# Unread products of ones behind the routing tables of the second and third token tile

## The chip, the cores and the metric

One core of a Trainium2 chip runs the whole program. The metric is the time of one execution on the device in microseconds, given as the median of several runs. Beside these runs there is one profiled execution, whose trace the rows below come from. All matrix products run on TensorE (PE in the profile); VectorE (DVE), ScalarE (ACT) and GpSimd (POOL) do the rest, and SyncE (SP) issues most transfers.

## What is computed

Two transformer blocks run one after the other on 512 tokens of width 1024. The first has a recurrent layer and a sliding-window layer, the second an mLSTM with a Fourier mixer. What this change touches is the end of the second block, where a hierarchical mixture of experts begins:

```
g_logits = h @ w_router_group + b          # 4 groups
g_sel    = argmax(g_logits)
e_sel    = (h @ w_router_expert + b) of that group    # 4 experts of it
top_v, top_i = top_k(e_sel, 2)
...
for e in range(16):
    a = silu(h @ w_gate[e]) * (h @ w_up[e])
    y = y + combine[..., e] * (a @ w_down[e])
```

The reference runs every expert on every token and weighs the results. The kernel computes each expert on the tokens routed to it alone, so it must first know the routes.

## The kernel before

The 512 tokens stand in four tiles of 128, t = 0 to 3. The stage around the change lies between the output projection of the mixer and the first expert.

`finish(t)` ends a tile of the mixer: it scales and adds the residual (line 1416, into `x3[t]`), lets ScalarE sum the squares of the result (line 1417), and for t below 3 transposes `x3[t]` on TensorE in two halves (`logits`, line 1398, copied out by ScalarE at line 1399) and multiplies it by the router's weights (line 1401). Of tile 3 most of this product was made earlier; what is left is one half of its `y`, transposed at the same line 1398. `finish(t)` also lets `h2(t - 1)` write the previous tile's rows to memory (line 1440), and makes the product with a row vector at line 1424. Last it calls `route`.

`route(t)` is a chain of some 30 small VectorE operations on the 20 logits of each token: it ranks groups and experts (lines 1567 to 1584), then TensorE counts how many earlier tokens went to each expert, in one group of three products (lines 1587, 1588 and 1589; the last, `self.ranked`, needs what line 1581 made). VectorE reads the count (line 1593), makes the one-hot rows by which the first expert's tokens are picked (line 1594) and two pairs of one-hot tables (lines 1609 and 1611), and two products at line 1612 add them into `self.tp`, the table of places. `self.tp` takes eight products over the four tiles.

After the third tile's ranks, `pick` (line 1546) multiplies the rows of tiles 0 to 2 by their one-hot rows, and after the fourth's those of tile 3: 32 products that give the first expert its tokens, already transposed. ScalarE and VectorE split them (lines 294 and 295), and the first expert's matrix products start (lines 303 to 305). The finished table gives the addresses (lines 1617 to 1619) by which the second expert's tokens are gathered from memory (line 1514). From then on 16 experts follow, each with three products per weight piece.

`warm(n)` makes n products of a 128x128 tile of ones with itself repeated (128x256 each), which nobody reads. It is used elsewhere in the program, where TensorE waits. `issue_after` asks the scheduler to place instructions behind a given one. The scheduler, not the code alone, decides in which order each engine's instructions stand.

Of the kernel before, what the change touches and what calls it, by code (L numbers as in the profile page):

```python
# [9 lines left out]
F32 = mybir.dt.float32  # L10
# [8 lines left out]
P = 128  # L19
T = 512  # L20
# [251 lines left out]
class Kern:  # L272
# [32 lines left out]
        self.last = mm(ps, lhsT=wl, rhs=xh, start=False, stop=stop)  # L305
        return self.last

    def warm(self, n, tag="at"):

        after = self.last  # L310
        ps = self.pps.tile([P, T], F32, name=tag, bufs=2)
        with self.tc.issue_after(after.ins):
            for _ in range(n):
                self.last = self.nc.tensor.matmul(ps[:, :2 * P], lhsT=self.ones,
                                                  rhs=self.ones[:, None, :].to_broadcast([P, 2, P]), start=True, stop=True)
# [1235 lines left out]
    def route(self, pc, lg, t):  # L1551

        nc = self.nc
        g, e = lg[:, 0:4], lg[:, 4:20].rearrange("p (g j) -> p g j", j=4)
        w = pc.tile([P, 153], F32, name="rtw", bufs=2)
        n = [0]

        def tw(*sh):
            k = math.prod(sh)
            n[0] += k  # L1560
            o = w[:, n[0] - k:n[0]]
            return o.rearrange("p (a b) -> p a b", a=sh[0]) if len(sh) == 2 else o

        def rank(x):

            d, r = tw(4, 4), tw(4)
            nc.vector.tensor_sub(d, x[:, None].to_broadcast([P, 4, 4]), x[:, :, None].to_broadcast([P, 4, 4]))
            nc.vector.tensor_tensor(d, d, self.c3("tie").rearrange("p (a b) -> p a b", a=4), op=ALU.is_gt)
            nc.vector.reduce_sum(r, d, axis=AX.X)
            return r  # L1570

        es, s = self.es[:, t], self.s12[:, t]
        gsel, em, s12 = tw(4), tw(4, 4), tw(4)
        nc.vector.tensor_scalar(gsel, rank(g), 0.0, None, op0=ALU.is_equal)
        gb = gsel[:, :, None].to_broadcast([P, 4, 4])
        nc.vector.tensor_mul(em, e, gb)
        nc.vector.reduce_sum(es, em.rearrange("p g j -> p j g"), axis=AX.X)
        r = rank(es)
        nc.vector.tensor_scalar(s12, r, 2.0, None, op0=ALU.is_lt)
        AA, A = tw(16), tw(2, 16)  # L1580
        nc.vector.tensor_mul(AA.rearrange("p (g j) -> p g j", j=4), gb, s12[:, None, :].to_broadcast([P, 4, 4]))
        for k in range(2):
            nc.vector.tensor_scalar(s[:, k], r, float(k), None, op0=ALU.is_equal)
            nc.vector.tensor_mul(A[:, k].rearrange("p (g j) -> p g j", j=4), gb, s[:, k, None, :].to_broadcast([P, 4, 4]))

        rp = self.pps.tile([P, 16], F32, name="mm", bufs=self.mmb)
        nc.tensor.matmul(rp, lhsT=self.ones, rhs=self.cum[:, t], start=True, stop=False)
        nc.tensor.matmul(rp, lhsT=self.ones[0:1], rhs=self.c3("eb")[0:1], start=False, stop=False)
        self.ranked = nc.tensor.matmul(rp, lhsT=self.c3("lt"), rhs=AA, start=False, stop=True)
        nc.vector.tensor_add(self.cum[:, t + 1], self.cum[:, t], AA)  # L1590

        p0 = tw(1)
        nc.vector.tensor_copy(p0, rp[:, 0:1])
        self.picked = nc.vector.tensor_scalar(self.oh0[:, t], self.c3("i128"), p0, AA[:, 0:1], op0=ALU.is_equal, op1=ALU.mult)
        m, val, rf = tw(2, 16), tw(2), tw(2, 2)
        nc.vector.tensor_mul(m, A, rp[:, None].to_broadcast([P, 2, 16]))
        ri = pc.tile([P, 3, 2], I32, name="ri", bufs=2)
        pos = tw(2)
        nc.vector.reduce_sum(pos, m, axis=AX.X)
        nc.vector.tensor_copy(ri[:, 0], pos)  # L1600
        nc.vector.tensor_scalar(ri[:, 1], ri[:, 0], 7, None, op0=ALU.logical_shift_right)
        nc.vector.tensor_scalar(ri[:, 2], ri[:, 0], P - 1, None, op0=ALU.bitwise_and)
        nc.vector.tensor_copy(rf, ri[:, 1:3])
        nc.vector.tensor_sub(val, self.c3("dest")[:, 2 * t:2 * t + 2], pos)

        oh = pc.tile([P, 2, 192], F32, name="oh", bufs=2)
        ohc, ohr = oh[:, :, :P], oh[:, :, P:]
        for k in range(2):
            nc.vector.tensor_scalar(ohr[:, k], self.c3("i64"), rf[:, 0, k:k + 1], val[:, k:k + 1], op0=ALU.is_equal,
                                    op1=ALU.mult)  # L1610
            nc.vector.tensor_scalar(ohc[:, k], self.c3("i128"), rf[:, 1, k:k + 1], None, op0=ALU.is_equal)
            nc.tensor.matmul(self.tp, lhsT=ohc[:, k], rhs=ohr[:, k], start=t + k == 0, stop=t + k == 4)

    def places(self):

# [460 lines left out]
```

## Time and profile before

| What | Value |
|---|---|
| median of 3 runs | 1872.26 us (1869.57 to 1874.68) |
| profiled execution, time | 1876.02 us |
| profiled execution, span of the trace | 1874.2 us |
| TensorE busy | 95% of the span |
| VectorE, ScalarE, GpSimd busy | 66%, 45%, 17% |
| mean granted clock of TensorE | 0.971 of full speed |

The span is what the trace covers, from the first instruction to the last; 1.8 us of the profiled time lie around it. The granted clock is 1.00 at TensorE's upper level of 2.4 GHz and 0.50 at the lower one of 1.2 GHz.

### The profile page before, as it was taken

How to read it: one execution, taken by the hardware profiler on the slowest of the kernel's cores; microseconds unless marked ns; L12 is line 12 of the kernel's file. 1: busy time of each engine (PE TensorE's matmuls, PEld its weight loads, DVE VectorE, ACT ScalarE, POOL GpSimd, SP SyncE). 2: the span in 40 equal slices, each digit the busy share in tenths (PEclk: the TensorE clock that was granted, in tenths of full speed). 3: DMA queues.
4: the chain of work that ended last, by engine and by line, in shares of the span. 5: the costliest groups of instructions: out<-in, count | busy, mean ns of one | idle time of the engine just before them, and what ended most of it. 6: DMA issues, size and time to landing. Idle time of an engine off the chain costs nothing.

```text
span 1874.2 us, 22970 instructions
## 1 busy us (share of the span) xinstructions
PE 1788.7 (95%) x8590; PEld 1447.1 (77%) x8590; DVE 1244.0 (66%) x2316; ACT 842.6 (45%) x1505; POOL 323.1 (17%) x251
## 2 busy tenths in 40 slices
PE   7899999999999999999999999988999889999995
PEld 5678788888888777777888888877877778888873
DVE  7854666577567665466645656568475698897897
ACT  6643432223234343434313222446454456786774
POOL 2300200000002100032000000222100024454543
PEclk9899999999999899999999999989999989999998
DMA  5212124334435411122343343301115359898883
GB/s 190 90 68 90 68 90 145 126 115 147 155 127 177 141 46 46 57 73 93 135 157 113 132 145 112 111 23 63 46 52 213 135 225 370 334 342 355 346 351 148
DMA packets 55257, 278.83 MB, mean 149 GB/s; under 512 B 7346, under 2 KB 16738, under 8 KB 28130
## 3 DMA queue, kind: packets, MB, share of 16 engines
q1 hardware_dynamic: 38146, 173.48, 26.6%
q0 software_dynamic: 16992, 103.82, 14.3%
q8 instruction: 69, 1.13, 0.2%
q14 instruction: 50, 0.41, 0.1%
HBM read 259.96 MB, written 17.32 MB: 148 GB/s over the span
## 4 chain that ended last, share of the span: by engine, by line
PE 83%; DVE 9%; ACT 2%; issue 1%; POOL 1%; DMA 1%; ACTq 0%; POOLq 0%; DVEq 0%
PE mm L303 22%; PE mm L305 22%; PE mm L304 22%; PE ax L641 2%; PE ax L396 1%; PE at L607 1%; PE ax L1749 1%; PE ax L625 1%; DVE h L453 1%; PE mm L1546 1%; PE dn L304 1%; PE ax L1401 1%; DVE elo L1509 1%; PE dn L303 0%; PE mm L986 0%
## 5 line engine op out<-in xcount | busy, mean ns | idle before, releaser
L303 PE MATMUL mm<-xh,whi 128*128 128x512 f32 x912 | 367.4, 404 | 11.6 <-ACT whi L294 8.1
L294 ACT CAST whi<-wraw 128x512 fp32r<-128x512 f32 x356 | 199.8, 607 | 395.6 <-DMA wraw<-w_fi_in 160.7
L304 PE MATMUL mm<-xl,whi 128*128 128x512 f32 (+1 forms) x944 | 373.9, 396 | 3.1 <-DVE xl L299 2.3
L295 DVE TENSOR_TENSOR wlo<-wraw,whi 128x512 fp32r<-128x512 f32 x352 | 240.3, 715 | 199.8 <-ACT whi L294 188.4
L305 PE MATMUL mm<-xh,wlo 128*128 128x512 f32 x912 | 363.0, 399 | 1.7 <-DVE wlo L295 1.7
L303 PEld LDWEIGHTS mm<-xh,whi 128*128 128x128 f32 x912 | 174.3, 191 | 56.7 <-ACT whi L294 9.8
L304 PEld LDWEIGHTS mm<-xl,whi 128*128 128x128 f32 x944 | 180.3, 191 | 44.5 <-DVE xl L299 4.5
L305 PEld LDWEIGHTS mm<-xh,wlo 128*128 128x128 f32 x912 | 174.1, 191 | 40.7 <-DVE wlo L295 2.9
L304 PE MATMUL mm<-al,whi 128*128 128x512 f32 (+1 forms) x520 | 201.1, 387 | 0.0
L303 PE MATMUL mm<-ah,whi 128*128 128x512 f32 x480 | 190.0, 397 | 0.7 <-ACT ah L294 0.7
L305 PE MATMUL mm<-ah,wlo 128*128 128x512 f32 x480 | 188.8, 394 | 0.0
L1509 DVE TENSOR_TENSOR elo<-wr,ehi 128x1024 fp32r<-128x1024 f32 x104 | 126.1, 1223 | 45.3 <-ACT ehi L1508 42.8
L440 POOL TENSOR_TENSOR acc<-acc,tmp 128x512 f32<-128x512 f32 (+1 forms) x50 | 67.0, 1339 | 434.1 <-ACT tmp L438 432.7
L304 PE MATMUL mm<-elo,X 128*128 128x512 f32 x352 | 138.6, 394 | 1.7 <-DVE elo L1509 1.5
L303 PE MATMUL mm<-ehi,X 128*128 128x512 f32 x352 | 138.0, 399 | 0.7 <-ACT ehi L1508 0.7
L305 PE MATMUL mm<-ehi,X 128*128 128x512 f32 x352 | 138.2, 393 | 0.0
L1508 ACT CAST ehi<-wr 128x1024 fp32r<-128x1024 f32 x104 | 108.7, 1052 | 61.5 <-PE mm L305 58.4
L515 POOL TENSOR_TENSOR tmp<-tmp 128x512 f32<-128x512 f32 x20 | 29.8, 1488 | 592.7 <-ACT tmp L509 437.2
L304 PEld LDWEIGHTS mm<-al,whi 128*128 128x128 f32 x520 | 99.3, 191 | 19.4 <-issue 0.8
L924 DVE SCALAR_TENSOR_TENSOR tmp<-wraw,silc,tmp 128x256 f32<-128x256 f32 x224 | 111.8, 532 | 1.9
L303 PEld LDWEIGHTS mm<-ah,whi 128*128 128x128 f32 x480 | 90.9, 190 | 23.1 <-issue 1.9
L305 PEld LDWEIGHTS mm<-ah,wlo 128*128 128x128 f32 x480 | 91.1, 190 | 19.6 <-issue 0.7
(550 smaller groups left out, 3131.3 us busy)
## 6 DMA issues: line engine op xcount, KB each, us to landing
wraw<-w_fi_in SPq DMA_DIRECT2D x44, 1024.0 KB
wraw<-w_ada_in SPq DMA_DIRECT2D x24, 1024.0 KB
wraw<-w_fo_in SPq DMA_DIRECT2D x16, 896.0 KB
wr<-w_ex_in SPq DMA_DIRECT2D x12, 1024.0 KB
wraw<-w_out_in SPq DMA_DIRECT2D x8, 1024.0 KB
wraw<-w_fo_in SPq DMA_DIRECT2D x8, 1024.0 KB
wraw<-w_in_a_in SPq DMA_DIRECT2D x5, 1024.0 KB
wraw<-w_mem_in SPq DMA_DIRECT2D x4, 1024.0 KB
```

The lines of the kernel that those rows point to most:

```text
L294: ins = nc.scalar.copy(hi, src)
L295: (eng or nc.vector).tensor_sub(lo, src, hi.bitcast(F32))
L303: mm(ps, lhsT=wh, rhs=xh, start=start, stop=False)
L304: mm(ps, lhsT=wh, rhs=xl, start=False, stop=False)
L305: self.last = mm(ps, lhsT=wl, rhs=xh, start=False, stop=stop)
L396: self.last = nc.tensor.matmul(ps[:, j * na + n:j * na + n + 1], lhsT=acc[:, j * P:(j + 1) * P], rhs=self.ones[:, 0:1], start=True, stop=True)
L440: nc.gpsimd.tensor_add(accs[0], accs[0], s)
L515: (nc.gpsimd if j % 2 else nc.vector).tensor_mul(t, t, gt.pop(j))
L641: nc.tensor.matmul(yb[:, n, r], lhsT=pts[n // 2][:, r, n % 2, b], rhs=x, start=b == vs[0][0], stop=b == 1)
L924: nc.vector.scalar_tensor_tensor(t, raw[:, k], s, t, op0=ALU.mult, op1=ALU.add)
L1508: self.split_hi = self.nc.scalar.copy(hi, src)
L1509: (eng or self.nc.vector).tensor_sub(lo, src, hi.bitcast(F32))
```

## The change

`route` now notes its last table product, and calls `warm` behind the tables of tiles 1 and 2 with six and eight products. They write a tile of the pool "mm" instead of "at", and `warm` takes the number of that pool's buffers.

```diff
-    def warm(self, n, tag="at"):
+    def warm(self, n, tag="at", bufs=2):
 
         after = self.last
-        ps = self.pps.tile([P, T], F32, name=tag, bufs=2)
+        ps = self.pps.tile([P, T], F32, name=tag, bufs=bufs)
         with self.tc.issue_after(after.ins):
             for _ in range(n):
                 self.last = self.nc.tensor.matmul(ps[:, :2 * P], lhsT=self.ones,
...
             nc.vector.tensor_scalar(ohc[:, k], self.c3("i128"), rf[:, 1, k:k + 1], None, op0=ALU.is_equal)
-            nc.tensor.matmul(self.tp, lhsT=ohc[:, k], rhs=ohr[:, k], start=t + k == 0, stop=t + k == 4)
+            self.last = nc.tensor.matmul(self.tp, lhsT=ohc[:, k], rhs=ohr[:, k], start=t + k == 0, stop=t + k == 4)
+        if t in (1, 2):
+            self.warm(4 + 2 * t, "mm", self.mmb)
```

Lines behind it have numbers two higher in the changed kernel. The order of instructions changes with it. On TensorE, behind the table of tile 0 (the first row), this is the difference; X_10742 is `x3[2]`, the products at line 1401 are the logits, L314 are the ones:

```order
 L1612 MATMUL ax<-oh 128x64 x2
+L1589 MATMUL mm<-rtw,cst_10714 128x16
+L1612 MATMUL ax<-oh 128x64 x2
+L314 MATMUL mm<-ones 128x256 x6
 L1398 MATMUL mm<-cst,X_10742 128x128 x8
+L1587 MATMUL mm<-acc_72,ones 128x16
+L1588 MATMUL mm<-cst_10714,ones 128x16
 L1401 MATMUL ax<-wrg,xg 128x20 x8
 L1589 MATMUL mm<-rtw,cst_10714 128x16
```

The rank product and the table of tile 1, which stood behind tile 2's transposes and logits, now stand ahead of them, and the six ones with them. The last row is the rank product of tile 1 before the change, and of tile 2 after it.

Behind that row TensorE goes on as follows; X_10813 is `y`, whose transposes belong to the logits of tile 3:

```order
+L1612 MATMUL ax<-oh 128x64 x2
+L314 MATMUL mm<-ones 128x256 x8
+L1398 MATMUL mm<-cst,X_10813 128x128 x4
 L1587 MATMUL mm<-acc_72,ones 128x16
 L1588 MATMUL mm<-cst_10714,ones 128x16
-L1398 MATMUL mm<-cst,X_10813 128x128 x4
+L1546 MATMUL mm<-oh_10822,X_10813 128x128 x3
 L1401 MATMUL ax<-wrg,xg 128x20 x4
-L1612 MATMUL ax<-oh 128x64 x2
+L1546 MATMUL mm<-oh_10822,X_10813 128x128 x21
 L1589 MATMUL mm<-rtw,cst_10714 128x16
```

Here the table of tile 2 and the eight ones stand ahead of the transposes and logits of tile 3, which before the change came ahead of the table of tile 1. The picks of tiles 0 to 2 (L1546) follow.

On VectorE this is the difference behind the third tile's one-hot rows; L1427 and L1428 take up the logits of tile 3, L376 to L380 are the small operations of its norm:

```order
 L1611 TENSOR_SCALAR oh<-cst_10714,rtw 128x128
+L1427 TENSOR_TENSOR lg<-lg,ax 128x20
+L1428 SCALAR_TENSOR_TENSOR lg<-lg,st,ax 128x20
+L1424 TENSOR_TENSOR X_10813<-X_10743,row 128x1024
+L376 TENSOR_SCALAR st<-st 128x1
+L377 RECIPROCAL st<-st 128x1
+L378 TENSOR_TENSOR st<-st 128x1
+L379 SCALAR_TENSOR_TENSOR st<-st 128x1
+L380 SCALAR_TENSOR_TENSOR st<-st 128x1
 L1434 SCALAR_TENSOR_TENSOR lg<-lg,st,cb 128x20
 L1440 SCALAR_TENSOR_TENSOR X_10813<-X_10813,st,row_10816 128x1024
```

These eight operations stood inside tile 2's route before; now they come behind it.

## Rows read from the trace of the kernel before

**Rows 1.** The page: the span, and TensorE's busy time, share and instructions.

```profile
span 1874.2 us, 22970 instructions
PE 1788.7 (95%) x8590; PEld 1447.1 (77%) x8590; DVE 1244.0 (66%) x2316; ACT 842.6 (45%) x1505; POOL 323.1 (17%) x251
```

**Rows 2.** Stretches, TensorE alone: length, busy (instructions), granted clock, DMA share, GB/s.

```profile
1487.50:1490.60 3.10, 0.00 (x0) 1.00 0.71 262
1492.40:1512.40 20.00, 15.23 (x68) 0.50 0.25 99
```

**Rows 3.** Chain that ended last: start, length, engine, line, count.

```profile
1483.20 0.80 PE ax L1401 x8
...
1492.20 3.60 PE ax L1401 x16
...
1507.40 2.00 PE mm L1546 x8
...
1514.46 3.00 PE mm L1546 x26
```

**Rows 4.** Timeline of TensorE; in brackets the idle time before.

```profile
1486.90 0.55 PE L1612 MATMUL ax<-oh 128*128 128x64 f32 x4
1490.64 1.07 PE L1398 MATMUL mm<-cst,X 128*128 128x128 f32 x8 [3.19 <-DVE rtw L1567]
...
1495.64 0.59 PE L1589 MATMUL mm<-rtw,cst 128*128 128x16 f32 x2
...
1505.83 0.61 PE L1589 MATMUL mm<-rtw,cst 128*128 128x16 f32 x2 [4.04 <-DVE rtw L1581]
...
1514.16 0.29 PE L1589 MATMUL mm<-rtw,cst 128*128 128x16 f32 x2
...
1518.34 0.48 PE L303 MATMUL mm<-ehi,X 128*128 128x512 f32 x1
```

**Rows 5.** Timeline of VectorE in the three routes.

```profile
1493.33 0.17 DVE L1581 TENSOR_TENSOR rtw<-rtw 128x16 f32<-128x16 f32 x1
...
1496.27 0.16 DVE L1593 COPY rtw<-mm 128x1 f32<-128x1 f32 x1 [2.44 <-PE mm L1589]
...
1498.31 0.28 DVE L1611 TENSOR_SCALAR oh<-cst,rtw 128x128 f32<-128x128 f32 x1
...
1500.99 0.16 DVE L1574 TENSOR_SCALAR rtw<-rtw 128x4 f32<-128x4 f32 x1
...
1504.26 1.22 DVE L1424 TENSOR_TENSOR X<-X,row 128x1024 f32<-128x1024 f32 x1
...
1508.83 1.28 DVE L1440 SCALAR_TENSOR_TENSOR X<-X,st,row 128x1024 f32<-128x1024 f32 x1
1510.03 0.17 DVE L1567 TENSOR_TENSOR rtw<-lg 128x16 f32<-128x16 f32 x1
...
1512.21 0.17 DVE L1581 TENSOR_TENSOR rtw<-rtw 128x16 f32<-128x16 f32 x1
...
1514.69 0.35 DVE L1594 TENSOR_SCALAR oh<-cst,rtw 128x128 f32<-128x128 f32 x1
```

**Rows 6.** Timeline of ScalarE: the copy of a transposed half.

```profile
1498.33 0.59 ACT L1399 COPY xg<-mm 128x512 f32<-128x512 f32 x1 [4.92 <-PE mm L1398]
```

**Rows 7.** Timeline of products of ones elsewhere (two records a product).

```profile
202.35 3.41 PE L314 MATMUL at<-ones 128*128 128x256 f32 x8
...
827.20 1.97 PE L314 MATMUL at<-ones 128*128 128x256 f32 x8
```

**Rows 8.** Stretches, TensorE alone, around the first of those (columns as in rows 2).

```profile
202.00:205.00 3.00, 3.00 (x9) 0.50 0.26 46
205.00:206.00 1.00, 1.00 (x7) 0.86 0.81 336
```

**Rows 9.** Chain that ended last: the gather of the second expert's tokens.

```profile
1520.87 5.67 DMA xg<-h2d,srci
```

**Rows 10.** Stretch of the experts: busy PE, PEld, DVE, ACT, POOL, clock, DMA share, GB/s.

```profile
1560.00:1800.00 240.00, 240.00 (x1139) 199.18 (x1138) 205.38 (x207) 177.27 (x207) 116.68 (x93) 1.00 0.91 352
```

## Prediction

> **What bounds the kernel now.** The page comes first: TensorE is busy 95% of the span [rows 1], so what counts is where it waits or runs slowly. In the stretch of the experts it is busy for all of 240 us at the upper level of its clock, and the DMA engines stand at 0.91 [rows 10]: nothing there ends before TensorE, so whatever delays the first expert delays the end by as much, and whatever brings it forward does the opposite.
>
> The stretches ahead of it show the place of the change. After the table of tile 0, which ends at 1487.45 (1486.90 + 0.55 [rows 4]), TensorE does nothing for 3.1 us, and from 1492.4 to 1512.4 the granted clock is 0.50, the lower level of 1.2 GHz [rows 2]. The chain of waits shows what this costs: eight records of the logits take 0.80 us at the upper level and sixteen take 3.60 at the lower, eight of the picks 2.00 and later twenty-six 3.00 [rows 3]. The timeline shows the waits for routes: 4.04 us ahead of the third tile's rank product [rows 4]. The first expert starts at 1518.34 [rows 4]. I call that start S and ask where it goes.
>
> **The change, step by step.** What the text of the change adds is 14 products, 28 records. Where ones ran at the upper level, eight records took 1.97 us with the last one's tail, 0.22 each [rows 7]. At the lower level I take twice that, 0.43. So six products are 2.6 us or 5.2, eight are 3.5 or 6.9.
>
> What weighs as much is where they stand. TensorE takes its products in the order given: in the rows of before the rank product of tile 1 begins at 1495.64 although line 1581 had its operand done at 1493.50, because sixteen records of logits stood ahead of it [rows 3 to 5]. After the change the rank product, table and ones of tile 1 stand ahead of tile 2's transposes, and the table and ones of tile 2 ahead of tile 3's. So I follow the new order with the old durations.
>
> 1. Tile 1's rank product no longer waits behind logits. It starts at 1493.55, 0.05 after its operand; TensorE stood idle for 6.1 us until then, so the clock is at the lower level, as it is in the rows of before [rows 2].
> 2. The count is read 0.64 later (1495.64 to 1496.27), the last one-hot row is done 2.3 after that (1496.27 to 1498.59), and I give the table's last product 0.5, near the 0.55 of a whole table [rows 4, 5]. Ones begin at 1497.0.
> 3. Six ones end at 1499.6 at the upper level and 1502.2 at the lower. Elsewhere the clock was still at 0.50 when ones began at 202.35 and rose at about 205.1, 2.8 us into them (0.86 in the stretch from 205 to 206) [rows 7, 8]. In the stage itself work resumed at 1505.83 and the clock rose at 1512.4, 6.6 us later [rows 2, 4]. Between these I take 4 us: nine records slow, three fast, end at 1501.6.
> 4. Only now come tile 2's transposes, which began at 1490.64 before [rows 4]. Four take 0.55, the copy 0.59 [rows 4, 6], sixteen records of logits 1.6, and 0.5 goes to the second copy and the hand-overs: 3.3 us at the upper level. At the lower it is 5.9, with the transposes doubled and the logits at 3.60. Tile 2's logits are ready at 1504.9 (bounds 1502.9 and 1508.1).
> 5. Tile 2's route up to its rank product. The ten small operations from line 1567 to the start of line 1581 took 2.18, 0.2 each, so the first four are about 0.9; from line 1574 to the rank product it was 4.84, of which 1.13 was line 1424 on the chain, which now stands elsewhere [rows 4, 5]. Together 4.6: 1509.5 (1507.5, 1512.7).
> 6. Count, one-hot rows and table as in step 2, 3.45 us: 1512.95 (1510.95, 1516.15). TensorE had nothing from 1504.9 to 1509.5, more than it had ahead of the first fall [rows 2], so I take the clock to be low again.
> 7. Eight ones: 4 us at the lower level hold nine records, seven more take 1.5; end at 1518.45. All fast it is 1514.45, all slow 1523.05.
> 8. Only now come the half of tile 3's logits and its route, which before ran beside the others. Transposes 0.55 and copy 0.59; counts and three picks go between, and the four logit products follow from 1.8 to 2.6 us. Then line 1427 at 2.7; lines 1428 and 1424 to 4.15; six small operations to 5.1; line 1440 to 6.35; from line 1567 to the rank product 2.4; from the rank product to the last pick's row 0.9 (1514.16 to 1515.04) [rows 4, 5]; eight picks, sixteen records at the 0.115 of the chain, 1.85 [rows 3]. With line 1567's part to 8.75, that is 9.65 and then 11.5 us. S is 1529.95 (1525.95, 1534.55), 11.6 us late (7.6, 16.2).
> 9. The gather was issued 2.5 us after S [rows 9]. The last table products now stand behind five products of the expert, and its first split stands ahead of tile 3's one-hot rows on VectorE; I take 0.8 us more (nothing to 1.2).
>
> The sum is +12.4 us. Set apart: with ones that cost nothing the same walk gives S at 1519.85, so 1.5 is the order alone, 6.1 the ones at the upper level, 4.0 the lower level under them, 0.8 the gather. On the profiled execution's 1876.02 us that is 1888.4. This execution lies 3.8 above the median of the runs, so I put the sum on the median: **1884.7 us**. What is taken away is one wait of 2.1 us (step 1), a wait for tile 3's logits on VectorE and line 1424's place in tile 2's route; all of it is in the walk. Behind S nothing gives it back, by the full stretch [rows 10]. Transfers that free buffers ask for move with S. The write of tile 3's rows moves with line 1440 and lands ahead of the gather.
>
> **The rivals.** The first is that ones don't hold up what stands behind them. It speaks for it that waits of 3.1 and 4.04 us are there to be filled [rows 2, 4]; against it is the rank product of tile 1, which was held up by 2.1 us in the same way. If later products passed the ones, the time would stay at 1872.3. The Trainium skill, "TensorE: Matmul & The Clock Gate", section "Step-by-step: what each phase is for", says that products stay in program order and only weight loads are pulled ahead; by that rule, with which the 2.1 us agree, this rival falls.
>
> The second ends on the other side: the ones lie inside the wait for tile 2's route, as the change has it in words. Then the clock is up when the route arrives, and eighteen pick records at 0.115 in place of 0.25 and ten records of ranks and tables at half their time give 2.4 + 1.0, 1868.9 us. It decides at one point: tile 2's transposes must start near 1490.6 as before. The changed order puts them behind six ones and a table, and against it is all of steps 1 to 4.
>
> The third is that the ones hold the clock at the upper level from their first record on, so that only their fast price is paid: 7.6 + 0.8, 1880.7 us. The idle stretches of 6.1 and 4.6 us ahead of them speak against it: the fall in the rows of before came behind a shorter one [rows 2]. The same page, section "Why this matters for your kernels", advises to leave no idle gap between bursts of products so that the clock stays up, which is the hope behind such ones; here the gaps stand in front of them, and the clock's fall behind the 3.1 us agrees with the advice.
>
> The fourth is that all ones, and tile 2's logits between them, run at the lower level: 16.2 + 0.8, 1889.3 us. The 6.6 us of step 3 speak for it.
>
> **How the numbers follow.** The forecast has 0.60, the clock held up 0.13, the lower level throughout 0.12, ones that hold nothing up 0.07, ones inside the wait 0.08. A measurement of this kernel tells about 0.3%, 5.6 us, from no change. The first three lie over it. Of the second rival half its chance lies within, at 1868.9 and above, and half below, where more of the slow stretch goes. So slower 0.85, same 0.11, faster 0.04. The range goes from 1878, the clock held up less the 2.7 us by which runs lie under the median, to 1891, the lower level throughout with 2 for the runs.
>
> **What would show it.** In the changed kernel's trace the rank product of tile 1 should follow 6 us of idle TensorE at 1493.5; twelve records of ones should lie between there and tile 2's transposes, which start after 1499; sixteen more should come after an idle stretch of over 4 us and ahead of tile 3's transposes; the clock should be at 0.50 when either group begins; the first expert should start some 12 us later, and the rest be the old trace shifted. I am wrong if the transposes of tile 2 still start near 1490.6, if either group runs at the upper level from its start, or if the stretch of the experts gets shorter by what S got later.

## The result, and the profile after

The changed kernel takes 1887.1 us (median of 7 runs, 1880.03 to 1890.73) against 1869.57 (7 runs, 1867.05 to 1874.68): ratio 1.0083, interval 1.0064 to 1.0102. It is slower by 12 to 19 us, 17.5 by the medians; 1884.7 had been forecast, within 1878 to 1891.

The page of the changed kernel hardly differs from [rows 1]:

```profile
span 1884.9 us, 23021 instructions
PE 1786.6 (95%) x8618; PEld 1443.9 (77%) x8618; DVE 1243.8 (66%) x2316; ACT 842.8 (45%) x1505; POOL 326.2 (17%) x251
```

There are 28 records more, yet TensorE's busy time is 2 us less, because stretches of low clock ahead of this stage differ from one execution to the next: up to the end of table 0 it was busy for 1436.8 us before and 1427.8 here, with 6940 records either time. The end of table 0 stood at 1487.45 in the first profile and at 1480.39 in this one, where nothing is changed up to there. So spans can't be subtracted; I count from the end of table 0.

The timeline of TensorE in the stage, which answers to [rows 4]:

```profile
1479.83 0.56 PE L1612 MATMUL ax<-oh 128*128 128x64 f32 x4
1486.50 0.61 PE L1589 MATMUL mm<-rtw,cst 128*128 128x16 f32 x2 [6.10 <-DVE rtw L1581]
1489.07 1.11 PE L1612 MATMUL ax<-oh 128*128 128x64 f32 x4 [1.96 <-DVE oh L1611]
1489.97 4.55 PE L314 MATMUL mm<-ones 128*128 128x256 f32 x12
1494.36 1.04 PE L1398 MATMUL mm<-cst,X 128*128 128x128 f32 x8
...
1495.78 1.96 PE L1401 MATMUL ax<-wrg,xg 128*128 128x20 f32 x16
1502.51 0.61 PE L1589 MATMUL mm<-rtw,cst 128*128 128x16 f32 x2 [4.77 <-DVE rtw L1581]
1505.08 1.11 PE L1612 MATMUL ax<-oh 128*128 128x64 f32 x4 [1.96 <-DVE oh L1611]
1505.98 5.94 PE L314 MATMUL mm<-ones 128*128 128x256 f32 x16
1511.76 0.60 PE L1398 MATMUL mm<-cst,X 128*128 128x128 f32 x4
...
1514.32 4.93 PE L1546 MATMUL mm<-oh,X 128*128 128x128 f32 x42
1520.60 0.40 PE L1589 MATMUL mm<-rtw,cst 128*128 128x16 f32 x2 [1.34 <-DVE rtw L1581]
1521.62 2.05 PE L1546 MATMUL mm<-oh,X 128*128 128x128 f32 x16 [0.63 <-DVE oh L1594]
1523.46 0.50 PE L303 MATMUL mm<-ehi,X 128*128 128x512 f32 x1
```

Both groups of ones stand between a table and the transposes (L1398) of a later tile, behind 6.10 and 4.77 us without a product. From the end of table 0 to the first expert, S, it is 43.07 us; it was 30.89. The stretches of TensorE alone show the clock (columns as in [rows 2]):

```profile
1489.97:1494.36 4.39, 4.39 (x13) 0.60 0.00 0
1494.36:1497.74 3.38, 3.38 (x29) 1.00 0.00 0
1505.98:1511.76 5.78, 5.78 (x18) 0.60 0.00 0
1511.76:1523.46 11.70, 9.73 (x84) 1.00 0.12 46
```

The granted clock means 0.60 in each group: low at first, up before the group ends (1.00 in the last 0.86 us of the first). What follows the ones runs at 1.00, where the logits and the first picks of before had 0.50 [rows 2, 3].

Behind S a second loss shows. In the chain that ended last, the gather, against 5.67 in [rows 9]:

```profile
1527.09 8.45 DMA xg<-h2d,srci
```

In TensorE's timeline, the transposes of the gathered rows:

```profile
1535.58 1.97 PE L1751 MATMUL ax<-cst,xg 128*128 128x128 f32 x8 [3.64 <-DMA xg<-h2d,srci]
```

And in the stretches of TensorE alone, what came next:

```profile
1535.58:1541.19 5.61, 5.61 (x17) 0.50 0.91 380
```

The gather was issued 3.63 us after S (2.53 before) and took 2.8 us longer; TensorE waited 3.64 us for it, the clock fell in that wait, and the products behind it ran at the lower level. The full stretch of the experts is that of [rows 10], only shifted:

```profile
1565.00:1805.00 240.00, 240.00 (x1136) 199.13 (x1135) 205.40 (x207) 177.77 (x207) 117.64 (x93) 1.00 0.91 352
```

### The profile page after: what moved, and what is told of

It is laid out like the page before. It is cut to its first block, busy times and chain, and to the rows that moved or that the text cites. A ratio compares the mean times of both kernels' runs of the same rounds, so it can differ in the third digit from the quotient of the medians.

```text
span 1884.9 us, 23021 instructions
## 1 busy us (share of the span) xinstructions
PE 1786.6 (95%) x8618; PEld 1443.9 (77%) x8618; DVE 1243.8 (66%) x2316; ACT 842.8 (45%) x1505; POOL 326.2 (17%) x251
## 4 chain that ended last, share of the span: by engine, by line
PE 83%; DVE 9%; ACT 2%; issue 1%; POOL 1%; DMA 0%; ACTq 0%; POOLq 0%; DVEq 0%
PE mm L303 22%; PE mm L305 22%; PE mm L304 22%; PE ax L641 2%; PE at L607 1%; PE ax L396 1%; PE ax L1751 1%; DVE h L453 1%; PE ax L625 1%; PE mm L314 1%; PE dn L304 1%; PE dn L303 0%; PE mm L986 0%; PE dn L305 0%; DMA xg<-h2d,srci 0%
## 5 line engine op out<-in xcount | busy, mean ns | idle before, releaser
L305 PEld LDWEIGHTS mm<-ah,wlo 128*128 128x128 f32 x480 | 90.4, 188 | 19.4 <-issue 0.7
```

## Experiments

All kernels in one table; after is the changed kernel. The four columns of times come from one profiled execution of each: the end of table 0 (start plus length of its last group), from there to S, from S to the first transposes of the gathered rows, and from there to the end of the span. The medians stand against those of the kernel before in the same comparison.

| kernel | table 0 ends | to S | to gather's transposes | to the end | median, before, ratio (interval) |
|---|---|---|---|---|---|
| before | 1487.45 | 30.89 | 8.24 | 347.62 | |
| before_again | 1484.15 | 30.14 | 8.13 | 347.58 | 1871.78, one run |
| after | 1480.39 | 43.07 | 12.12 | 349.32 | 1887.1, 1869.57, 1.0083 (1.0064 to 1.0102) |
| after_again | 1483.14 | 44.18 | 9.96 | 348.82 | 1888.23, 1868.86, 1.0113 (1.0094 to 1.0132) |
| one_each | 1487.67 | 39.72 | 10.09 | 348.82 | 1881.51, 1868.66, 1.0070 (1.0047 to 1.0093) |
| double | 1485.46 | 51.04 | 8.78 | 348.92 | 1896.13, 1868.66, 1.0143 (1.0114 to 1.0172) |
| first | 1480.80 | 33.81 | 12.04 | 349.45 | 1877.45, 1870.25, 1.0035 (1.0017 to 1.0053) |
| second | 1483.26 | 35.44 | 8.97 | 348.93 | 1878.27, 1870.25, 1.0062 (1.0039 to 1.0084) |
| spare | 1481.21 | 32.51 | 7.48 | 348.80 | 1872.45, 1868.66, 1.0022 (1.0005 to 1.0039) |
| spare01 | 1479.78 | 25.79 | 9.82 | 347.51 | 1869.52, 1868.66, 1.0006 (0.9987 to 1.0024) |
| spare0 | 1482.14 | 27.79 | 7.99 | 347.78 | 1870.38, 1870.25, 1.0000 (0.9980 to 1.0020) |
| spare65 | 1480.12 | 25.34 | 9.44 | 347.60 | 1866.11, 1868.86, 0.9995 (0.9978 to 1.0012) |
| behind | 1485.18 | 44.07 | 9.10 | 362.45 | 1902.78, 1870.25, 1.0176 (1.0157 to 1.0194) |

My theory: the ones stand in the path in program order, so that the stage pays for their place and their length. Its rival: they fill a wait and the time goes elsewhere. The first four runs ask which.

**one_each**, one product behind each of the two tables:

```diff
-            self.warm(4 + 2 * t, "mm", self.mmb)
+            self.warm(1, "mm", self.mmb)
```

> One product of ones behind each of the two tables in place of six and eight, written to the same pool, so the order of the other products is that of the change. If the loss of the change is the sum of its order and of ones in series (the forecast), 12 of 14 products go: about 8 us less at the first expert's start, given back in part because nothing lifts the clock while tile 2's logits run. So 6 to 13 us over the kernel before, against 17.5 for the change. If the order alone costs it: about 17.5 again. If ones alone cost it: within 2 us of the kernel before.

It lost 12.9 us by the medians, though only 2 of the 14 products are left. So the larger part is not the length of the ones. The timeline:

```profile
1497.09 1.17 PE L314 MATMUL mm<-ones 128*128 128x256 f32 x2
1498.05 1.92 PE L1398 MATMUL mm<-cst,X 128*128 128x128 f32 x8
...
1500.67 3.60 PE L1401 MATMUL ax<-wrg,xg 128*128 128x20 f32 x16
1509.04 0.61 PE L1589 MATMUL mm<-rtw,cst 128*128 128x16 f32 x2 [4.77 <-DVE rtw L1581]
```

The order is the changed kernel's, with 5.94 and 4.77 us of idle (6.10 and 4.77 there); with few ones the logits run at the lower level, 3.60 us in place of 1.96. Long groups cost more themselves and give part of it back.

**double**, twelve and sixteen products:

```diff
-            self.warm(4 + 2 * t, "mm", self.mmb)
+            self.warm(8 + 4 * t, "mm", self.mmb)
```

> Twelve and sixteen products of ones in place of six and eight, same order. If the ones stand in series on the path to the first expert, each further product costs its time at the upper level, 0.43 us: 14 x 0.43 = 6.1 us more than the change, about 23.5 over the kernel before. If they lie in waits or the order alone costs: no more than the change, 17.5.

It lost 27.5 us by the medians (interval 21 to 32), 10 more than the change, where 6.1 more were the forecast. S came 7 to 8 us later than in the two profiles of the changed kernel. The longer groups of ones account for 5.6 to 6.7 of that, so added ones lie on the path in full. The last picks account for another 1.4: behind a wait of 0.64 us they ran at a granted clock of 0.53 and took 3.50 us, not the 2.05 of the changed kernel.

```profile
1494.88 7.32 PE L314 MATMUL mm<-ones 128*128 128x256 f32 x24
...
1513.65 9.89 PE L314 MATMUL mm<-ones 128*128 128x256 f32 x32
...
1533.25 3.50 PE L1546 MATMUL mm<-oh,X 128*128 128x128 f32 x16 [0.64 <-DVE oh L1594]
```

From the end of table 0 to the end the profile is only 4.2 and 5.8 us longer than those of the changed kernel, because the gather was not late here. What else went into the 10 us of the medians stays open.

**spare**, the same products behind the same tables, written to unread columns of the table's own tile instead of a tile of the pool "mm":

```diff
-        self.tp = self.pps.tile([P, 64], F32, name="ax", bufs=2)
+        self.tpw = self.pps.tile([P, T], F32, name="ax", bufs=2)
+        self.tp = self.tpw[:, :64]
...
-            self.warm(4 + 2 * t, "mm", self.mmb)
+            self.warm(4 + 2 * t, open_=self.tpw[:, 2 * P:])
```

Given `open_`, `warm` writes there and neither starts nor closes an accumulation.

> Six and eight ones behind the same two tables, but added into unread columns of the table's own tile, so that they take no buffer of the pool that tile 2's transposes use; the transposes and logits of tiles 2 and 3 then stand where they stood before the change, and six ones fall in the wait of 4.0 us ahead of tile 2's rank product. If the place of the ones is what costs (the forecast): between 3 us faster and 3 us slower than the kernel before, since twelve records fill that wait at the lower level with 1 us too many and lift the clock for the picks. If ones cost their time wherever they stand: 10 us slower.

4 us by the medians, interval 1 to 7: just over the range. On TensorE the order of all other products up to the picks is that of the kernel before, with 3.19 us of idle ahead of tile 2's transposes as in [rows 4]; the ones follow the tables where these stood:

```profile
1484.40 1.94 PE L1398 MATMUL mm<-cst,X 128*128 128x128 f32 x8 [3.19 <-DVE rtw L1568]
...
1494.65 1.09 PE L1613 MATMUL ax<-oh 128*128 128x64 f32 x4
1495.54 5.43 PE L314 MATMUL ax<-ones 128*128 128x256 f32 x12
1500.76 0.45 PE L1590 MATMUL mm<-rtw,cst 128*128 128x16 f32 x2
```

So which tile the ones write decides where later products stand, and that place is the larger part of the 17.5 us. Why the pool moves them I read from the code alone: the ones take one of the pool's six buffers ahead of the later tiles' transposes, which take theirs from the same pool.

**spare01**, **spare0**, **spare65**: ones in spare columns in the idle time behind table 0 (six), with eight, none or five behind table 1; the diff is spare01's against spare. They ask whether the aim of such ones can be had.

```diff
-        if t in (1, 2):
-            self.warm(4 + 2 * t, open_=self.tpw[:, 2 * P:])
+        if t in (0, 1):
+            self.warm((6, 8)[t], open_=self.tpw[:, 2 * P:])
```

> As the run before it, but six ones behind the table of tile 0, in the idle 3.1 us ahead of which the clock fell, and eight behind the table of tile 1; none behind tile 2. Six at the upper level are 2.6 us, so they end before tile 2's transposes can start. If the clock then stays up, sixteen records of logits take 1.6 us in place of 3.6, and the later ranks, logits and picks go at twice the speed: 4 to 7 us faster than the kernel before. If VectorE's chain sets the pace of the stage: within 2 us of the kernel before.

> Six ones in unread columns of the table's own tile behind table 0 alone; none elsewhere; the order is that of the kernel before. They fill the 3.19 us of idle ahead of tile 2's transposes, so the transposes and logits of tile 2 run at the upper level (1.96 us for sixteen records in place of 3.60) and tile 1's rank product comes up to 3 us sooner. After that the wait for tile 2's route is there as before and the clock falls in it. Theory: the first expert 2 to 5 us earlier, time 0 to 5 us under the kernel before, about 1866. Rival: the clock falls all the same a little later, as it did in the kernel with ones behind tables 0 and 1, and what is won is lost under the picks: no change.

> The kernel with ones in spare columns behind tables 0 and 1, with five products behind table 1 in place of eight: in the kernel with eight, tile 2's rank product came 0.7 us later after table 0's end than its place in the kernel without them would allow, so that the last of them were in its way. Theory: ones end before tile 2's rank product's operand is ready, the clock is up for the picks, the first expert comes 25 us after table 0 (25.8 with eight, 27.8 with none, 30.9 before) and the time is 3 to 6 us under the kernel before, 1863 to 1866. Rival: a gain in this stage doesn't show in the time, as with the other two, 1868 to 1871.

In the profiles the stage got shorter by about as much as expected: S came 2.7 us (spare0), 4.7 (spare01) and 5.2 (spare65) sooner than the mean of the two profiles of before. The clock of before fell behind the idle 3.1 us, and not ahead of them as the first of these expectations has it: in them it was still 1.00 [rows 2]. Spare0's timeline shows the logits of tile 2 at the upper level and those of tile 3's half, 4 us later, at the lower one again:

```profile
1481.98 2.81 PE L314 MATMUL ax<-ones 128*128 128x256 f32 x12
...
1486.90 1.96 PE L1401 MATMUL ax<-wrg,xg 128*128 128x20 f32 x16 [0.49 <-ACT xg L1399]
...
1491.13 1.90 PE L1401 MATMUL ax<-wrg,xg 128*128 128x20 f32 x8 [0.73 <-ACT xg L1399]
...
1497.99 0.61 PE L1590 MATMUL mm<-rtw,cst 128*128 128x16 f32 x2 [4.04 <-DVE rtw L1582]
```

The times don't confirm a gain: all three intervals hold 1. For spare0 and spare65 they don't rule out the 2.7 and 3.9 us by which the profiles are shorter from table 0 to the end, since their intervals reach down to 3.7 and 4.1 us under the kernel before. In spare01 and spare65 1.3 to 1.6 us of it go to a gather whose transposes come 9.4 to 9.8 us after S, not 8.2. The Trainium skill, "TensorE: Matmul & The Clock Gate", section "Why this matters for your kernels", advises to leave no gaps between bursts of products. The 1.96 us in place of 3.60 agrees; the clock's fall soon after, with no wait over 0.73 us since the ones began, does not, and no gain that can be measured came of it here.

**first** and **second**: the changed kernel with only one of its two groups.

```diff
-        if t in (1, 2):
+        if t == 1:
```

> The changed kernel with only the six ones behind tile 1's table; the eight behind tile 2's table are left out. Theory of the walk: the start is that of the changed kernel (6.1 us idle, table, ones 4.4 us, ones' end 14.0 us after the end of table 0), the logits of tile 2 and half of tile 3's follow, the rank product of tile 2 stands some 22 us after table 0 (18.4 before), and the rest of the stage takes about the 12.5 us it took before, since tile 3's logits are ready early again. So the first expert is some 4 us late and the time is 2 to 7 us over the kernel before, most likely 4.5, 1873. Rival, that each product adds the same wherever it stands: six of the fourteen, so 7.5 us of the 17.5.

> The changed kernel with only the eight ones behind tile 2's table; the six behind tile 1's table are left out. Theory of the walk: up to the rank product of tile 2 all is as before (18.4 us after table 0 or a little less), 3.5 us on to the ones, ones 4.5 to 6 us, then the 11.7 us from the end of the ones to the first expert that the changed kernel's trace shows, because tile 3's transposes stand behind them: the first expert 7 to 9 us late, the gather about 1 us more, time 8 to 11 us over the kernel before, about 1878. With the six alone this makes some 14 of the 17.5 us. Rival, that each product adds the same: eight of fourteen, 10 us, which this kernel can't tell from the theory by its time; its trace does, since the theory puts half of it behind the ones and not under them. Rival, that ones in the wait for tile 3's route cost nothing: no change.

Six alone cost 3 to 10 us by the ratio, eight alone 7 to 16; the medians say 7.2 and 8.0, where 2 to 7 and 8 to 11 were expected. Together that is 15.2, near the 17.5. The times alone would also fit the rival that each product adds the same (7.5 and 10); one_each, which lost 12.9 us with two products, does not. The rank product of tile 2 in TensorE's timeline, first's above and second's below:

```profile
1501.76 0.44 PE L1589 MATMUL mm<-rtw,cst 128*128 128x16 f32 x2 [1.19 <-DVE rtw L1581]
```

```profile
1498.56 0.61 PE L1589 MATMUL mm<-rtw,cst 128*128 128x16 f32 x2 [3.40 <-DVE rtw L1581]
```

For the six the walk held: rank product of tile 2 21.0 us after table 0 (22 expected), S 3.3 us late (4 expected); the rest of the loss stands behind S. For the eight S was 4.9 us late, not 7 to 9: without the six, tile 2's rank product came 15.3 us after table 0 instead of 18.4. VectorE's part of tile 2's route no longer holds three things that it held before, and that I had left out: a wait of 0.47 us for ScalarE's step of tile 3's norm, one of 1.47 us for tile 3's logits, and the 1.13 us of line 1424. The waits in VectorE's timeline of before:

```profile
1499.14 0.15 DVE L376 TENSOR_SCALAR st<-st 128x1 f32<-128x1 f32 x1 [0.47 <-ACT st L375]
...
1500.90 0.18 DVE L1427 TENSOR_TENSOR lg<-lg,ax 128x20 f32<-128x20 f32 x1 [1.47 <-PE ax L1401]
```

With both groups this gain is lost behind the six ones (rank product 22.1 us after table 0), so in the stage 3.3 and 4.9 do not add up to the change's 13.1. Of second's loss 7.0 us are in its profile.

**behind** asks whether the weights' loads make the gather late.

```diff
-            early = [fetch(j, 1, odd(j), nc.gpsimd if j > 3 else nc.sync) for j in range(6)]
+            with tc.issue_after(self.gathered.ins):
+                early = [fetch(j, 1, odd(j), nc.gpsimd) for j in range(6)]
```

Here `gathered` is the gather's instruction.

> The changed kernel with the six early loads of the second expert's weights all on the GpSimd queue and behind the first gather, in place of four on the sync queue and two on the GpSimd queue with one of them ahead of the gather. Theory that the gather landed late (8.45 us after its issue in place of 5.67) because those loads were on the way: the gather lands 5 to 6 us after its issue, TensorE waits under 1 us for it, the clock doesn't fall there, and the time is 3 to 5 us under the changed kernel, 1882 to 1884. Rival, that the gather's landing scatters by itself or is held up by the first expert's own loads on the sync queue, which stay: 6 to 8.5 us as it comes, time that of the changed kernel, 1887, or over it where the second expert's weights come late.

The time was not 3 to 5 us under the changed kernel but 32.5 over the kernel before, by the medians. The gather's transposes came 5.37 us after its issue, but that decides nothing: double and second had 5.19 and 5.33 with the loads where they were. The loads now came late, and ScalarE waited for them (line, total, times, longest), with some 13 us more than in the changed kernel between these transposes and the end:

```profile
ACT ehi L1508 <- DMA h<-w_ex_in: 6.6, 2, 3.5
```

**after_again** and **before_again** are the two kernels unaltered, for second profiles.

> The changed kernel unaltered, for a second profiled execution. Theory that the late first gather of the first profile (8.45 us from issue to landing, 3.6 us of wait, then 1.7 us of slow products) came by chance, since the same order gave 5.2 to 6.4 us in other kernels: the first expert is 12 us late against the end of table 0 as before, the gather issued 3.6 us after its start, but landing in 5 to 6.5 us, so that the stretch from the end of table 0 to the end is some 13 to 14 us longer than before (not 17.75); the time stays 12 to 19 us above the kernel before. Rival, that the landing belongs to this order: 8.4 us again.

> The kernel before unaltered, for a second profiled execution: the stretch from the end of table 0 to the first expert 30.9 us again if it is set by the order alone, and the first gather 5 to 8.5 us from issue to landing if that scatters in this order too (5.67 if it does not). The part of the program ahead of table 0's end, 1487 us in the first profile, between 1480 and 1488.

The stage repeats: 44.18 and 30.14 us. The time does too, 19.4 us over the kernel before by the medians (interval 18 to 25; 12 to 19 expected). The gather does not; its transposes stood this close behind their wait:

```profile
1537.28 1.09 PE L1751 MATMUL ax<-cst,xg 128*128 128x128 f32 x8 [1.49 <-DMA xg<-h2d,srci]
```

That is 6.33 us after the issue in place of 8.49, and no fall of the clock. The stretch from table 0 to the end is 402.96 us, 16.7 more than the mean of the two profiles of before (386.30); 18.2 in the first profile. I had expected 13 to 14.

## Why the prediction was right, and where a term was off

The steps are those of the prediction, and the times those of the first profile of the changed kernel unless another is named.

- **Steps 1 and 2**, the order: 6.10 us of idle (6.1 forecast), 3.47 from the rank product to the ones (3.45).
- **Steps 3 and 7**, the ones: 4.39 and 5.78 us, 10.2 together, where 6.1 at the upper level and 4.0 for the lower make 10.1. The clock rose inside each group, between the third and the fourth rival. That it fits so closely is luck: step 3 chose 4 us between two readings, 2.8 and 6.6 (the first should be 2.9, since its 0.86 puts the rise at about 205.3, not 205.1). In after_again the groups took 5.13 and 6.15, 11.3 together. There the first stood at the lower level almost to its end, as the fourth rival has it; but what came behind them had 1.00, as in the first profile (after_again's stretches, columns as in [rows 2]):

```profile
1492.71:1497.84 5.13, 5.13 (x13) 0.51 0.00 0
1497.84:1501.22 3.38, 3.38 (x29) 1.00 0.00 0
...
1509.46:1515.61 6.15, 6.15 (x17) 0.57 0.00 0
```

- **Steps 4 to 6**: 3.38 us to the end of tile 2's logits (3.3), 4.77 of idle (4.6), 3.47 to the second ones (3.45).
- **Step 8**: 11.70 us from the ones' end to S (11.5). The stage came out 12.2 us longer (11.6 forecast), 13.1 between the means of the two profiles each.
- **Step 9** is the term that was mis-sized, 0.8 us for the gather. The issue moved by 1.1, within the bound of 1.2. Its transposes came 3.9 and 1.8 us later after S than before, and behind them another 1.7 and 1.2 went: in the first profile to the slow products, in the second to a stretch of low clock 294 us later, near the end of the experts, which the first profile of before does not have (last section). So the rest was not just the old trace shifted. Behind S that is 5.6 and 3.0 us. I had carried over 5.67 us for the landing as if it were fixed; in kernels whose order is that of the change it was 5.2 to 8.5.
- **The base**: the sum of 12.4 stood on a median of 1872.26; over seven runs it was 1869.57. The sum was 5 us short of the 17.5, the base 2.7 too high. These errors point opposite ways, so that the forecast lies only 2.4 us from the time is luck.
- **"Order 1.5, ones 6.1, lower level 4.0"** as separate shares did not hold. One_each has the order with hardly any ones (two, 1.9 us), and S is 9.2 us late, not 1.5: the 1.5 had put all that follows the ones at the upper level, and without long groups to raise the clock the logits and many of the picks run slowly. From there the change adds twelve products, 8.3 us of TensorE's time, and S moves by 3.4 to 4.5 more. The total stood because the walk had both effects in it; the order's share is the larger.

Of the rivals, the first and the second fall by the timeline: no product passed the ones, and tile 2's transposes didn't start as before. Ones that leave the order alone, as in spare, cost 4 us and not a gain.

What stays open: what makes the gather land 2 to 3 us later in some executions, and whether it does so more often in the new order. In three profiles with the order of before around the gather (before, before_again, spare0) its transposes came 5.5 to 5.7 us after the issue, in eight profiles of the other order 5.2 to 8.5 (behind not counted, nor spare, where TensorE did not wait for it).

## What to carry to other kernels

Before products that nobody reads are put into a wait, see in the order of the built program whether they stand in it: the tile that they write competes for its pool's buffers with later work, and the work that moves behind them can cost more than they do. Here the same 14 products in the same lines of code cost 17.5 us with one tile and 4 with another. Where a clock falls in long waits, as here behind 3.1 to 6.1 us, fillers are priced at both levels, and at their end the path, not the engine's busy share, says whether the faster clock gave it back.

## What had not been expected of the hardware

- The upper level that ones kept up did not last: in spare0 the clock was 1.00 under the ones and in the stretch 1485.34 to 1488.70, and 0.50 from 1490 to 1491, with no wait over 0.73 us since the ones began. In TensorE's stretches:

```profile
1485.34:1488.70 3.36, 2.87 (x24) 1.00 0.99 413
1488.70:1490.00 1.30, 1.30 (x12) 0.95 0.82 321
1490.00:1491.00 1.00, 0.40 (x2) 0.50 0.05 16
```

- The same waits can be followed by either level. Near the end of the experts TensorE waits 1.32 and 0.61 us in after_again as in before; the products behind had 0.54 in the one and 1.00 in the other (one_each, double and second had a low stretch there too, spare0 and before_again none). In TensorE's stretches, after_again's first, then before's:

```profile
1831.98:1835.34 3.36, 3.36 (x8) 0.54 0.01 2
```

```profile
1821.23:1824.07 2.84, 2.69 (x10) 1.00 0.02 9
```

- The transposes of one gather in the same place came 5.2 to 8.5 us after its issue, from kernel to kernel and between two executions of the same kernel (8.49 and 6.33).
- The unchanged part ahead of table 0's end took between 1479.8 and 1487.7 us in thirteen profiles, a spread of 7.9 us. By the medians five of the ten altered kernels moved the time by no more than that.
